# A per-row skewness kernel: row-to-partition mapping, load widths and the closing of the last two blocks

## The chip, the cores and the metric

The kernel runs on one core of a Trainium2 chip. The metric is the device time of one execution in microseconds (us), lower is better. Thirteen runs of the kernel before are at hand, and one profiled execution of it.

The engines named below: TensorE (PE, with its weight loads shown apart as PEld), VectorE (DVE), ScalarE (ACT), GpSimd (POOL) and SyncE (SP), which here only issues DMA transfers. SBUF is the memory on the chip that all of them reach; PSUM is the one into which PE writes.

## The reference

```python
rows, cols = 1024, 8192                      # x is float32, normally distributed
mean = np.mean(x, axis=-1, keepdims=True)
std = np.std(x, axis=-1, keepdims=True)
z = (x - mean) / (std + 1e-8)
return np.mean(z ** 3, axis=-1)              # 1024 numbers
```

For each row the kernel needs three means: m1 of x, m2 of x squared, m3 of x cubed. With var = m2 - m1², the answer is (m3 - 3·m1·(var + m1²/3)) · var^(-1.5); the two inner terms are 3·m1·m2 - 2·m1³ written differently. x is 33.55 MB and is read once.

## The kernel before, in words

The 1024 rows are eight blocks of 128; row 128b+p of x goes to partition p of block b. A block is 8192 columns wide and is loaded in *units*, whose widths are listed in `UNITS`: four for block 0 (512, 1024, 2560, 4096), two each for blocks 1 to 3, then three, four, five, and nine for block 7 (1152 four times, 1024, 896, 896, 512, 256). There are 31 units, so 31 loads, all issued in order by SP. One unit is 128 row pieces, one for each partition. Eight unit buffers rotate (`X_BUFS = 8`): the load of a unit is issued when the unit eight places before it has been read by PE, ACT and DVE.

Work on a unit, cut into slices of at most 2304 columns (`SUB_MAX`), goes in this order:

- ACT squares a slice (`sq`, line 135), with a scale that makes the sum along the row a share of m2. The sum goes to one column of `s2u` (or of `s2l` in block 7).
- DVE multiplies `sq` by x (line 139), and the sum, a share of m3, goes to one column of `s3u` (or `s3l`). DVE waits for ACT's slice.
- PE sums x itself: it transposes each 128 columns and accumulates all of them in one PSUM tile `tp` (line 145). At the end of a block ACT copies `tp` to `tsb` (line 115), and a matmul with a column of 1/8192 leaves m1 of the block in column b of `s1ps` (line 116).

The slices of the last two units of block 7 have their `sq` in PSUM and their cube in a scratch tile `cubes`.

Blocks 0 to 6 are closed together after block 6 (`finish_first_blocks`): two reductions on DVE (line 97), three small ACT instructions (lines 101 to 103), six on POOL. Block 7 is closed at the end: ACT sums `s2l` (line 156), then squares m1, and forms `var`, `nm1` and `v3` from it (lines 160 to 165); POOL raises `var` to the power -1.5 (line 163); DVE reduces `s3l` (line 157), combines it with `v3` and `nm1` (line 166) and multiplies by the power (line 169). The 128x8 tile `skew` is then transposed on PE (line 172), copied out of PSUM by DVE (line 174), and stored by one DMA of eight pieces of 512 bytes (line 175).

The engines run their own instructions in order. A scheduler places the instructions that are written near one another, so the order on an engine may differ a little from that of the source.

Of the kernel before, what the change touches and what calls it, by code (L numbers as in the profile page):

```python
# [8 lines left out]
FP = mybir.dt.float32  # L9
AF = mybir.ActivationFunctionType  # L10
ALU = mybir.AluOpType
X_AXIS = mybir.AxisListType.X


UNITS = [
    [512, 1024, 2560, 4096],
    [4096, 4096],
    [4096, 4096],
    [4352, 3840],
    [3328, 2816, 2048],  # L20
    [2048, 2048, 2048, 2048],
    [1792, 1792, 1664, 1536, 1408],
    [1152, 1152, 1152, 1152, 1024, 896, 896, 512, 256],
]
SUB_MAX = 2304
X_BUFS = 8
SQ_BUFS = 4
PSUM_SQ = 2


def _slices(w):
    n = -(-w // SUB_MAX)
    step = -(-w // n // 128) * 128
    return [(s, min(s + step, w)) for s in range(0, w, step)]


@with_exitstack
def kernel(
    ctx: ExitStack,
    tc: tile.TileContext,  # L40
    x: bass.AP,
    out: bass.AP,
):
    nc = tc.nc
    P = nc.NUM_PARTITIONS
    R, C = x.shape
    NB = R // P
    L = NB - 1
    inv_n = 1.0 / float(C)
    s_scale = float(C) ** -0.5  # L50
    third = (1.0 / 3.0) ** 0.5
    assert len(UNITS) == NB and all(sum(u) == C for u in UNITS)

    xv = x.rearrange("(b p) c -> b p c", p=P)
    ob = out.rearrange("(b p) -> b p", p=P)


    n_sub = [sum(len(_slices(w)) for w in u) for u in UNITS]
    MAXC = max(n_sub[:L])
    NL = n_sub[L]  # L60

    xpool = ctx.enter_context(tc.tile_pool(name="xp", bufs=X_BUFS))
    sqpool = ctx.enter_context(tc.tile_pool(name="sqp", bufs=SQ_BUFS))
    onep = ctx.enter_context(tc.tile_pool(name="onep", bufs=1))
    psum = ctx.enter_context(tc.tile_pool(name="ps", bufs=2, space=bass.MemoryType.PSUM))
    psq = ctx.enter_context(tc.tile_pool(name="psq", bufs=2, space=bass.MemoryType.PSUM))
    psum1 = ctx.enter_context(tc.tile_pool(name="ps1", bufs=1, space=bass.MemoryType.PSUM))

    onesn = onep.tile([P, 1], FP, tag="onesn")
    nc.vector.memset(onesn, inv_n)  # L70
    tiny = onep.tile([P, 1], FP, tag="tiny")
    nc.scalar.activation(out=tiny, in_=onesn, func=AF.Square)  # L72
    ident = onep.tile([P, P], FP, tag="ident")
    make_identity(nc, ident)
    s2u = onep.tile([P, L * MAXC], FP, tag="s2u")
    s3u = onep.tile([P, L * MAXC], FP, tag="s3u")
    nc.vector.memset(s2u, 0.0)
    nc.vector.memset(s3u, 0.0)
    s2l = onep.tile([P, NL], FP, tag="s2l")
    s3l = onep.tile([P, NL], FP, tag="s3l")  # L80
    cubes = onep.tile([P, 512], FP, tag="cubes")
    junk = onep.tile([P, NL], FP, tag="junk")
    expo = onep.tile([P, L], FP, tag="expo")
    nc.gpsimd.memset(expo, -1.5)
    skew = onep.tile([P, NB], FP, tag="skew")
    s1ps = psum1.tile([P, NB], FP, tag="s1ps")

    Tsb = [onep.tile([P, P], FP, tag=f"tsb{i}", name=f"tsb{i}") for i in range(2)]

    def small(name, n):  # L90
        return onep.tile([P, n], FP, tag=name, name=name)

    def finish_first_blocks():

        m2, m3 = small("m2a", L), small("m3a", L)
        for dst, src in ((m2, s2u), (m3, s3u)):
            nc.vector.tensor_reduce(  # L97
                out=dst, in_=src.rearrange("p (b c) -> p b c", c=MAXC), axis=X_AXIS, op=ALU.add
            )
        m1sq, m1sq3, nm1 = small("m1sqa", L), small("m1sq3a", L), small("nm1a", L)  # L100
        nc.scalar.activation(out=m1sq, in_=s1ps[:, 0:L], func=AF.Square)
        nc.scalar.activation(out=m1sq3, in_=s1ps[:, 0:L], func=AF.Square, scale=third)
        nc.scalar.activation(out=nm1, in_=s1ps[:, 0:L], func=AF.Copy, scale=-3.0)
        g = nc.gpsimd
        var, rr = small("vara", L), small("rra", L)
        g.tensor_tensor(out=var, in0=m2, in1=m1sq, op=ALU.subtract)  # L106
        g.tensor_tensor(out=m1sq3, in0=m1sq3, in1=var, op=ALU.add)  # L107
        g.tensor_tensor(out=m1sq3, in0=m1sq3, in1=nm1, op=ALU.mult)  # L108
        g.tensor_tensor(out=m3, in0=m3, in1=m1sq3, op=ALU.add)  # L109
        g.tensor_tensor(out=rr, in0=var, in1=expo, op=ALU.pow)  # L110
        g.tensor_tensor(out=skew[:, 0:L], in0=m3, in1=rr, op=ALU.mult)  # L111

    def close_block(b, tp):
        tsb = Tsb[b % 2]
        nc.scalar.copy(out=tsb, in_=tp)  # L115
        nc.tensor.matmul(out=s1ps[:, b : b + 1], lhsT=tsb, rhs=onesn, start=True, stop=True)  # L116

    for b, widths in enumerate(UNITS):
        last = b == L
        tp = psum.tile([P, P], FP, tag="tp", name=f"tp_{b}")  # L120
        c0 = 0
        j = 0
        for k, w in enumerate(widths):
            xt = xpool.tile([P, w], FP, tag="x", name=f"x_{b}_{k}")
            nc.sync.dma_start(out=xt, in_=xv[b, :, c0 : c0 + w])
            c0 += w
            for s, e in _slices(w):
                i = b * MAXC + j
                a2 = s2l[:, j : j + 1] if last else s2u[:, i : i + 1]
                a3 = s3l[:, j : j + 1] if last else s3u[:, i : i + 1]  # L130
                j += 1
                in_psum = last and k >= len(widths) - PSUM_SQ
                pool = psq if in_psum else sqpool
                sq = pool.tile([P, e - s], FP, tag="sq", name=f"sq_{b}_{k}_{s}")
                nc.scalar.activation(  # L135
                    out=sq, in_=xt[:, s:e], func=AF.Square, scale=s_scale, accum_out=a2
                )
                cube = cubes[:, 0 : e - s] if in_psum else sq
                nc.vector.scalar_tensor_tensor(  # L139
                    out=cube, in0=sq, scalar=1.0, in1=xt[:, s:e],  # L140
                    op0=ALU.mult, op1=ALU.mult, accum_out=a3,
                )
            n = w // P
            for c in range(n):
                nc.tensor.matmul(  # L145
                    out=tp, lhsT=xt[:, c * P : (c + 1) * P], rhs=ident,
                    start=(k == 0 and c == 0), stop=(c0 == C and c == n - 1),
                    is_transpose=True,
                )
        close_block(b, tp)  # L150
        if b == L - 1:
            finish_first_blocks()


    m2, m3 = small("m2l", 1), small("m3l", 1)
    nc.scalar.activation(out=junk, in_=s2l, func=AF.Copy, accum_out=m2)
    nc.vector.tensor_reduce(out=m3, in_=s3l, axis=X_AXIS, op=ALU.add)  # L157
    m1sq, var, nm1, v3 = small("m1sql", 1), small("varl", 1), small("nm1l", 1), small("v3l", 1)
    p1 = s1ps[:, L:NB]
    nc.scalar.activation(out=m1sq, in_=p1, func=AF.Square)  # L160
    nc.scalar.activation(out=var, in_=m1sq, func=AF.Identity, scale=-1.0, bias=m2)  # L161
    rr = small("rrl", 1)
    nc.gpsimd.tensor_tensor(out=rr, in0=var, in1=expo[:, 0:1], op=ALU.pow)  # L163
    nc.scalar.activation(out=nm1, in_=p1, func=AF.Copy, scale=-3.0)
    nc.scalar.activation(out=v3, in_=m1sq, func=AF.Identity, scale=1.0 / 3.0, bias=var)
    nc.vector.tensor_scalar(  # L166
        out=m3, in0=v3, scalar1=nm1, scalar2=m3, op0=ALU.mult, op1=ALU.add
    )
    nc.vector.tensor_tensor(out=skew[:, L:NB], in0=m3, in1=rr, op=ALU.mult)  # L169

    skT_ps = psum1.tile([NB, P], FP, tag="skT")
    nc.tensor.matmul(out=skT_ps, lhsT=skew, rhs=ident, start=True, stop=True, is_transpose=True)  # L172
    skT = small("skT", P)[0:NB, :]
    nc.vector.tensor_copy(out=skT, in_=skT_ps)  # L174
    nc.sync.dma_start(out=ob, in_=skT)


# [28 lines left out]
```

## Time and profile before

| What | Value |
|---|---|
| median of 13 runs | 93.29 us (92.28 to 93.66) |
| profiled execution | 93.07 us |
| its span, first to last instruction | 91.3 us |
| outside the span | 1.8 us |
| instructions | 1437 |
| granted TensorE clock, mean | 0.993 |
| DMA loads | 31, 33.55 MB |
| output store issued at | 89.21 us of the span |

The profile's page gives the busy time of each engine, a strip of 40 slices of the span with the busy share in tenths, and groups of instructions with their mean duration, the idle time just ahead of them, and what ended that idle time. Other views of the same trace are used below: who waited for whom, and the timeline, which lists instructions with start, duration, engine, line, operation, output and inputs, and in brackets the idle time before them with what ended it.

### The profile page before, as it was taken

What the parts mean: (1) busy time and instruction counts of PE and PEld (TensorE: products, weight loads), DVE (VectorE), ACT (ScalarE), POOL (GpSimd) and SP (SyncE); (2) the same over time, 40 slices, a digit from 0 to 9 for tenths busy, and PEclk for the clock granted to TensorE, in tenths of its full rate; (3) what the DMA queues carried; (4) which work ended last, traced back from release to release, by engine and by line L of the source; (5) the groups of instructions that cost most, each with busy time, mean ns of one, the idle gap of its engine ahead of it and who ended that gap; (6) DMA issues with size and microseconds to landing.
All of it is one profiled execution on the core that took longest, in us unless ns stands there. A gap on an engine that the chain in (4) does not pass through costs nothing. (4 is left out here: it accounts for less than half of the span.)

```text
span 91.3 us, 1437 instructions
## 1 busy us (share of the span) xinstructions
PE 68.3 (75%) x529; PEld 60.8 (67%) x529; DVE 73.8 (81%) x91; ACT 69.3 (76%) x101; POOL 9.4 (10%) x14
## 2 busy tenths in 40 slices
PE   0480898979495949779298998887789798989610
PEld 0360897979493939678297897877678687867500
DVE  0142290898989798987969999999999999999960
ACT  6350827969595959779399999977798899999830
POOL 3000000000000000000000000000000000699820
PEclk9999999999999999999999999999999999999997
DMA  1999999999999999999999999999999999992000
GB/s 41 357 346 448 438 438 402 445 438 438 395 445 438 441 408 450 399 424 432 407 428 415 433 409 413 434 403 412 422 417 414 412 409 414 413 364 99 0 0 2
DMA packets 4486, 33.64 MB, mean 369 GB/s; under 512 B 504, under 2 KB 640, under 8 KB 2560
## 3 DMA queue, kind: packets, MB, share of 16 engines
q1 hardware_dynamic: 4480, 33.56, 88.9%
q8 instruction: 4, 0.07, 0.3%
q14 instruction: 2, 0.02, 0.0%
HBM read 33.55 MB, written 0.00 MB: 368 GB/s over the span
## 5 line engine op out<-in xcount | busy, mean ns | idle before, releaser
L139 DVE SCALAR_TENSOR_TENSOR sq<-sq,x 128x2048 f32<-128x2048 f32 (+11 forms) x39 | 71.5, 1884 | 13.9 <-ACT sq L135 13.9
L145 PE MATMUL tp<-ident,x 128*128 128x128 f32 x512 | 65.5, 285 | 15.0 <-DMA x<-in_x_dram 14.7
L135 ACT ACTIVATE sq<-x 128x2048 f32<-128x2048 f32 (+12 forms) x41 | 62.9, 1534 | 17.1 <-DMA x<-in_x_dram 16.1
L145 PEld LDWEIGHTS tp<-ident,x 128*128 128x128 f32 x512 | 59.0, 147 | 20.3 <-DMA x<-in_x_dram 16.8
L106 POOL TENSOR_TENSOR vara<-m2a,m1sqa 128x7 f32<-128x7 f32 x1 | 1.3, 1293 | 77.0 <-DVE m3a L97 77.0
L135 ACT ACTIVATION_READ_ACCUMULATOR sq<-x 128x1 f32 x41 | 7.6, 186 | 0.0
L116 PEld LDWEIGHTS s1ps<-onesn,tsb 128*128 128x128 f32 x16 | 2.4, 188 | 5.5 <-ACT tsb L115 5.5
L116 PE MATMUL s1ps<-onesn,tsb 128*128 128x1 f32 x16 | 3.1, 261 | 3.6 <-ACT tsb L115 3.6
L139 DVE DVE_READ_ACCUMULATOR sq<-sq,x 128x1 f32 x39 | 3.2, 82 | 0.0
L110 POOL TENSOR_TENSOR rra<-vara,expo 128x7 f32<-128x7 f32 x1 | 2.6, 2622 | 0.0
L115 ACT COPY tsb<-tp 128x128 f32<-128x128 f32 x8 | 2.0, 252 | 0.1
L72 ACT ACT_TABLE_LOAD x1 | 1.3, 1283 | 0.7 <-PEq L190 0.7
L172 PE MATMUL skT_ps<-ident,skew 128*8 128x128 f32 x1 | 0.3, 273 | 2.0 <-DVE skew L169 2.0
L172 PEld LDWEIGHTS skT_ps<-ident,skew 128*8 128x8 f32 x1 | 0.1, 83 | 2.1 <-DVE skew L169 2.1
L107 POOL TENSOR_TENSOR m1sq3a<-m1sq3a,vara 128x7 f32<-128x7 f32 x1 | 1.2, 1202 | 0.1
L139 DVE SCALAR_TENSOR_TENSOR cubes<-sq,x 128x512 f32<-128x512 f32 (+1 forms) x2 | 1.1, 554 | 0.1
L108 POOL TENSOR_TENSOR m1sq3a<-m1sq3a,nm1a 128x7 f32<-128x7 f32 x1 | 1.1, 1150 | 0.0
L109 POOL TENSOR_TENSOR m3a<-m3a,m1sq3a 128x7 f32<-128x7 f32 x1 | 0.9, 935 | 0.1
L111 POOL TENSOR_TENSOR skew<-m3a,rra 128x7 f32<-128x7 f32 x1 | 0.9, 933 | 0.1
L70 DVE MEMSET onesn<- 128x1 f32 x1 | 0.1, 59 | 0.8 <-PEq L190 0.8
L163 POOL TENSOR_TENSOR rrl<-varl,expo 128x1 f32<-128x1 f32 x1 | 0.6, 561 | 0.6 <-ACT varl L161 0.6
L174 DVE COPY skT<-skT_ps 8x128 f32<-8x128 f32 x1 | 0.3, 279 | 0.4 <-PE skT_ps L172 0.4
(25 smaller groups left out, 4.4 us busy)
## 6 DMA issues: line engine op xcount, KB each, us to landing
x<-in_x_dram SPq DMA_DIRECT2D x5, 2048.0 KB, 18.8
x<-in_x_dram SPq DMA_DIRECT2D x5, 1024.0 KB, 25.1
x<-in_x_dram SPq DMA_DIRECT2D x4, 576.0 KB, 9.8
x<-in_x_dram SPq DMA_DIRECT2D x1, 2176.0 KB, 34.1
x<-in_x_dram SPq DMA_DIRECT2D x1, 1920.0 KB, 37.6
x<-in_x_dram SPq DMA_DIRECT2D x2, 896.0 KB, 14.8
x<-in_x_dram SPq DMA_DIRECT2D x1, 1664.0 KB, 34.9
x<-in_x_dram SPq DMA_DIRECT2D x1, 1408.0 KB, 31.3
```

Source lines behind the costliest of these rows:

```text
L72: nc.scalar.activation(out=tiny, in_=onesn, func=AF.Square)
L106: g.tensor_tensor(out=var, in0=m2, in1=m1sq, op=ALU.subtract)
L107: g.tensor_tensor(out=m1sq3, in0=m1sq3, in1=var, op=ALU.add)
L108: g.tensor_tensor(out=m1sq3, in0=m1sq3, in1=nm1, op=ALU.mult)
L109: g.tensor_tensor(out=m3, in0=m3, in1=m1sq3, op=ALU.add)
L110: g.tensor_tensor(out=rr, in0=var, in1=expo, op=ALU.pow)
L111: g.tensor_tensor(out=skew[:, 0:L], in0=m3, in1=rr, op=ALU.mult)
L115: nc.scalar.copy(out=tsb, in_=tp)
L116: nc.tensor.matmul(out=s1ps[:, b : b + 1], lhsT=tsb, rhs=onesn, start=True, stop=True)
L135: nc.scalar.activation(out=sq, in_=xt[:, s:e], func=AF.Square, scale=s_scale, accum_out=a2)
L139: nc.vector.scalar_tensor_tensor(out=cube, in0=sq, scalar=1.0, in1=xt[:, s:e], op0=ALU.mult, op1=ALU.mult, accum_out=a3,)
L145: nc.tensor.matmul(out=tp, lhsT=xt[:, c * P : (c + 1) * P], rhs=ident, start=(k == 0 and c == 0), stop=(c0 == C and c == n - 1), is_transp ...
```

## The change

- **Rows.** Partition p of block b now holds row 8p+b. Neighbouring partitions of one load are 8 rows apart in memory (256 KB in place of 32 KB). The eight results of a partition are neighbours in the output, and `skew` is stored directly by one DMA of 128 pieces of 32 bytes. The transpose, the copy and their tiles are gone.
- **Widths.** `UNITS` has 27 units: 4096 wide in blocks 0 to 3, then shrinking, and 1024 to 1408 in block 7, the last one 1152. The last unit alone has its `sq` in PSUM.
- **Row sums on ACT.** In the first unit of blocks 0, 1 and 2 the last 1024 columns are summed by an ACT copy with a row sum (`S1_ACT`, line 159) and no longer by PE: 24 transposes fewer. The two parts of m1 are added by DVE (line 177).
- **Closing.** Blocks 0 to 5 are closed together after block 5, in the same manner as seven were. Blocks 6 and 7 are closed with a chain of six small ACT instructions each (`close_on_act`); for block 6 it is spread between the squares of block 7. The last of the six writes v3·nm1 (the m1 term of the numerator) into a spare column of `s3u`, so that one reduction over `s3u` gives both numerators. One POOL power and one DVE multiplication then serve both blocks.

```diff
 UNITS = [
-    [512, 1024, 2560, 4096],
-    [4096, 4096],
-    [4096, 4096],
-    [4352, 3840],
-    [3328, 2816, 2048],
-    [2048, 2048, 2048, 2048],
-    [1792, 1792, 1664, 1536, 1408],
-    [1152, 1152, 1152, 1152, 1024, 896, 896, 512, 256],
+    [4096, 4096],
+    [4096, 4096],
+    [4096, 4096],
+    [4096, 4096],
+    [3584, 2304, 2304],
+    [2304, 2304, 2048, 1536],
+    [1664, 1792, 1920, 1664, 1152],
+    [1024, 1024, 1152, 1280, 1408, 1152, 1152],
 ]
+S1_ACT = {(0, 0): 1024, (1, 0): 1024, (2, 0): 1024}
-PSUM_SQ = 2
+EARLY = 6
...
-    xv = x.rearrange("(b p) c -> b p c", p=P)
-    ob = out.rearrange("(b p) -> b p", p=P)
+    xv = x.rearrange("(p b) c -> b p c", b=NB)
+    ov = out.rearrange("(p b) -> p b", b=NB)
...
+    def close_on_act(b):
+        m2, m1sq, nm1, v3 = (small(f"{t}_{b}", 1) for t in ("m2", "m1sq", "nm1", "v3"))
+        p1 = s1ps[:, b : b + 1]
+        var = var2[:, b - F : b - F + 1]
+        act = nc.scalar.activation
+        yield act(out=junk, in_=s2u[:, b * K : b * K + K], func=AF.Copy, accum_out=m2)
+        yield act(out=m1sq, in_=p1, func=AF.Square)
+        yield act(out=var, in_=m1sq, func=AF.Identity, scale=-1.0, bias=m2)
+        yield act(out=nm1, in_=p1, func=AF.Copy, scale=-3.0)
+        yield act(out=v3, in_=m1sq, func=AF.Identity, scale=1.0 / 3.0, bias=var)
+        yield act(
+            out=s3u[:, b * K + K - 1 : b * K + K], in_=v3, func=AF.Identity, scale=nm1
+        )
...
+            w_act = S1_ACT.get((b, k), 0)
+            if w_act:
+                nc.scalar.activation(
+                    out=same[:, 0:w_act], in_=xt[:, w - w_act : w], func=AF.Copy,
+                    scale=inv_n, accum_out=s1a[:, b : b + 1],
+                )
+            n = (w - w_act) // P
...
+            if k > 0:
+                next(pending, None)
+                next(pending, None)
...
+        if b == F - 2:
+            nc.vector.tensor_tensor(
+                out=m1a[:, 0:nw], in0=s1ps[:, 0:nw], in1=s1a, op=ALU.add
+            )
+        if b == F - 1:
+            close_first_blocks()
+        if b >= F:
+            pending = close_on_act(b)
+    for _ in pending:
+        pass
+    rr = small("rr2", NB - F)
+    nc.gpsimd.tensor_tensor(out=rr, in0=var2, in1=expo[:, 0 : NB - F], op=ALU.pow)
+    num = small("num2", NB - F)
+    nc.vector.tensor_reduce(
+        out=num, in_=s3u[:, F * K :].rearrange("p (b c) -> p b c", c=K), axis=X_AXIS, op=ALU.add
     )
...
-    nc.tensor.matmul(out=skT_ps, lhsT=skew, rhs=ident, start=True, stop=True, is_transpose=True)
-    skT = small("skT", P)[0:NB, :]
-    nc.vector.tensor_copy(out=skT, in_=skT_ps)
-    nc.sync.dma_start(out=ob, in_=skT)
+    nc.vector.tensor_tensor(out=skew[:, F:NB], in0=num, in1=rr, op=ALU.mult)
+    nc.sync.dma_start(out=ov, in_=skew)
```

## The prediction

> **What bounds the kernel now.** I read the page's strip of 40 slices first, to see which engine is full and when.
>
> ```profile
> DVE  0142290898989798987969999999999999999960
> ...
> DMA  1999999999999999999999999999999999992000
> GB/s 41 357 346 448 438 438 402 445 438 438 395 445 438 441 408 450 399 424 432 407 428 415 433 409 413 434 403 412 422 417 414 412 409 414 413 364 99 0 0 2
> ```
>
> The DMA engines are full from the second slice to the 36th: the loads never pause. DVE has gaps in the first half and none in the second. The waits, asked for two windows (up to 47 us and after), say the same. The columns are the total, how many, and the longest.
>
> ```profile
> DVE sq L139 <- ACT sq L135: 13.2, 9, 3.5
> ```
> ```profile
> DVE sq L139 <- ACT sq L135: 0.7, 1, 0.7
> ```
>
> DVE's waits for ACT are ACT's waits for data, passed on; the last one ends at 47.05. From the timeline, the rows that carry the sums:
>
> ```profile
> 9.43 4.53 PE L145 MATMUL tp<-ident,x 128*128 128x128 f32 x20 [2.52 <-DMA x<-in_x_dram]
> ...
> 45.09 3.50 PE L145 MATMUL tp<-ident,x 128*128 128x128 f32 x30 [1.77 <-DMA x<-in_x_dram]
> ...
> 47.05 2.16 DVE L139 SCALAR_TENSOR_TENSOR sq<-sq,x 128x1920 f32<-128x1920 f32 x1 [0.71 <-ACT sq L135]
> ...
> 59.78 1.97 PE L145 MATMUL tp<-ident,x 128*128 128x128 f32 x16 [0.30 <-DMA x<-in_x_dram]
> ```
> ```profile
> 83.92 1.40 PEld L145 LDWEIGHTS tp<-ident,x 128*128 128x128 f32 x13 [0.33 <-DMA x<-in_x_dram]
> ...
> 85.92 0.24 ACT L115 COPY tsb<-tp 128x128 f32<-128x128 f32 x1
> ...
> 86.63 0.17 ACT L160 ACTIVATE m1sql<-s1ps 128x1 f32<-128x1 f32 x1 [0.27 <-PE s1ps L116]
> ...
> 87.16 0.29 ACT L165 ACTIVATE v3l<-m1sql,varl 128x1 f32<-128x1 f32 x1
> ...
> 87.72 0.16 DVE L157 TENSOR_REDUCE m3l<-s3l 128x1 f32<-128x9 f32 x1
> ...
> 88.38 0.16 DVE L169 TENSOR_TENSOR skew<-m3l,rrl 128x1 f32<-128x1 f32 x1
> 88.59 0.08 PEld L172 LDWEIGHTS skT_ps<-ident,skew 128*8 128x8 f32 x1 [2.08 <-DVE skew L169]
> ...
> 89.21 0.37 SPq L175 DMA_DIRECT2D out_dram<-skT  x1
> ```
>
> A PE row that waited for DMA starts when a unit has landed. 45,056 columns are there at 59.78, 64,768 at 83.92: 24.14 us / 19,712 = 1.2246 ns a column, 512 bytes each, 418 GB/s. Going back on that line, 32,768 columns are due at 44.73 (seen: 45.09) and 4,096 at 9.62 (seen: 9.43), so one line serves the whole kernel, and all 65,536 have landed at 83.92 + 768 × 1.2246 ns = 84.86. DVE's pace is read from starts that follow one another in the timeline: 57.94 to 60.15 for 2048 columns, 79.46 to 80.74 for 1152, so 0.084 us an instruction and 1.038 ns a column, 15% faster than the data. DVE therefore works off the lag that wide units give it. The path is: data up to 45.09, ACT's first slice, DVE without a gap from 47.05 to 87.69 (40.6 us), then a tail of 1.5 us to the store at 89.21 and 2.1 us more to the end of the span.
>
> **The change part by part.**
>
> *Start.* The small first units go. DVE then starts at about 11.5 in place of 4.16. This costs nothing: what covers it is the later wait for data, which DVE has at every unit up to 47.05. What could gain is the stream: slices 2 and 3 run at 357 and 346 GB/s against 440 later, so (83 + 94) GB/s × 2.28 us = 0.40 MB or 0.9 us is lost there. If the small transfers are the reason, it comes back; if it is a run-in of the queue, nothing does. Bounds 0 and -0.9; I take -0.3, nearer to the run-in, since 1152-wide loads later keep 413 GB/s.
>
> *ACT sums three times 1024 columns* (nearest row: 1024-wide square, 1.06 us and 0.19 for its sum). ACT needs 2 × 1.91 for a 4096 unit, which comes every 5.02; 3.82 + 1.1 still fits. PE has 24 transposes fewer (0.12 us each: 32 take 3.71), but PE waits for data there anyway. Both cost nothing; without the cover the three copies would be 3.2 us. The eight buffers need no new wait: SP already waits for a buffer (22 waits for DVE) while the DMA row stays full, and the last seven units hold 8,192 columns, 10 us of stream.
>
> *DVE to the end.* Both kernels have landed 32,768 columns with the second unit of block 3. Taking 45.09 again, ACT's first slice (2048, 1.91) and 0.15 of handing over let DVE start at 47.15. It then has 36,864 columns in 22 instructions: 38.27 + 1.85, plus 0.24 for the two reductions (line 97 before, now after block 5) and 0.12 for line 177: end 87.63. The rest before was 36,608 columns in 25 instructions. So DVE by itself ends where it ended.
>
> *ACT in blocks 6 and 7.* This is the new load. After block 5 and again after block 6, ACT now waits in its own order for PE's `s1ps` before the next square; in the tail of before the same step took 85.92 to 86.63. Queued behind it are the squares, and behind these DVE. For block 6: 0.71 for copy and wait, 0.07, then 0.42 for var, nm1, v3 (v3 started 0.53 after m1sq), 0.08 for the s3u column: 1.3 us. ACT's free time in block 7 is the data's pace less its own: 1024 wide 1.25 - 1.06, 1152 wide 1.41 - 1.17, 1280 and 1408 wide about 0.30 and 0.35, together 1.5 us up to the last unit. So ACT is late by over 1 us at the second unit of block 7 and just on time at the last one. DVE, which by then has no lag left, loses some 0.3 us in short waits. End of the cubes about 87.9. The other bound agrees: last data 84.86, square 1.17, handing over 0.15, cube 1.35 + 0.08: 87.6.
>
> *Tail.* The last square ends at about 86.07, 0.2 us after the last one of before (the 256-wide piece, 85.89). From the `tsb` copy at 86.1, v3 starts 1.24 later (85.92 to 87.16), the new column 0.33 after that and takes 0.29: ready at 87.96. The one reduction starts at 88.0, bounded by ACT and DVE alike (before 87.72). From there: reduce 0.16, gap 0.1, multiply 0.16, 0.04 to the issue: 88.5. Before it was 89.21, since line 166 (0.38 with its gap) and transpose and copy (88.55 to 89.21) stood in between. POOL's power of two columns (0.56 for one) waits for var at 87.3 and is ready at 88.0, hidden. POOL's six for the first blocks move some 9 us earlier, clear of it. Sum: -0.7.
>
> *Store.* 8 pieces of 512 bytes become 128 of 32. The trace has the nearest row on the load side: the first load, 128 pieces of 2 KB on an idle queue, lands 2.6 us after its issue, of which 0.6 us is its 256 KB at 418 GB/s; the other 2.0 is no more than the 2.1 of the store. By that row the piece count costs nothing. The Trainium skill, "DMA: Bandwidth & Descriptors", section "Specifications", speaks against it: a piece under 512 B is written by reading and modifying. Its HBM access latency is 0.2 us on average ("Latency and other measured facts"); with 8 pieces on each of 16 engines one after another my estimate from the page is 1.6 us. Below zero there is little to find: the store must still be issued and land. I take +0.3, near the row.
>
> *Row pitch.* All loads now step 256 KB from partition to partition; the trace has 32 KB alone, at 418 GB/s, and by that row nothing changes. The skill's rule speaks against: the same page, section "Latency and other measured facts", has copies of 128 × 16 KiB tiles at 207 GB/s with a 512 KiB pitch, 164 at 2 MiB, 103 at 4 MiB, and about 214 unhindered. 3.3% of the 80.2 us of stream (33.55 MB at 418) is 2.6 us, an estimate for twice our pitch, so an upper bound; half an effect would be 1.3. No row shows that another pitch is better, but a little gain isn't excluded. I take 0, since the fall is small at 512 KiB and shrinks with the pitch, and keep 2.6.
>
> Sum on the profiled execution: start -0.3, tail -0.7 (the later end of the cubes is in it), store +0.3, pitch 0: -0.7, so the span goes from 91.3 to 90.6 and the time from 93.07 to about 92.4. That execution lies 0.2 below the median of the 13; against 93.29 it is 92.6.
>
> **The rivals.**
>
> *The pitch slows the stream* (slower side). Place: every load. Price: 0.8 us for each percent. It eats the gain at 0.9%, 414 GB/s in place of 418, and is slower by over 0.5% from about 1.5%. At the page's 3.3%: 92.6 + 2.6 = 95.2. For it: the kernel hangs on the stream from end to end, with PE and ACT waiting at unit after unit. Against: the pitch before is a power of two as well and costs nothing visible.
>
> *ACT's chains eat the gain.* If each dependent small instruction costs its 0.33 and the wait for PE 0.7 twice, block 6's closing is 2.1 us against 1.5 free; the last square starts 0.5 us late, everything after it too, and with a store at +0.5 the time is 93.3. For it: order on ACT puts m1sq ahead of block 7's first square. Against: in before, three such ACT instructions (lines 101 to 103) took 0.17 together.
>
> *The start gives its full 0.9 us* and the store costs nothing: 93.29 - 0.7 - 0.9 = 91.7.
>
> **How the numbers follow.** A measurement of this kernel can tell about 0.5% (0.47 us) from no change. Forecast (around 92.6): 0.38, of which 0.05 within 0.5%. Pitch: 0.28, of which 0.03 within. ACT and store: 0.18, of which 0.08 within, 0.08 slower, 0.02 faster. Start in full: 0.16, all faster. Faster 0.33 + 0.02 + 0.16 = 0.51; within 0.16; slower 0.25 + 0.08 = 0.33. The likeliest case alone is 92.0 to 93.1. The range goes from 91.5 (beyond the full start by a little) to 95.2 (the page's pitch figure).
>
> **What would show it.** Right: GB/s near 430 from the second slice; 32,768 columns landed at about 44.8, the last unit at 84.5; DVE full from about 47; short DVE waits in block 7; the reduction on line 190 waiting for ACT's column at about 87.7, 0.5 us from there to the store's issue, and 2.1 to 2.4 more to the end. Wrong: landings drifting behind 1.2246 ns a column (pitch); ACT's squares of block 7 starting over 0.3 us after their data at the last unit (chains); over 2.6 us from the store's issue to the end (store).

## The result, and the profile after

The changed kernel takes 91.46 us (median of 11 runs, 91.37 to 91.65), the kernel before 93.22 (48 runs, 92.06 to 93.91). The medians differ by 1.76 us. The ratio, for which runs over 1.5% above the fastest of the same kernel are left out, is 0.9856, with a 95% interval of 0.9825 to 0.9886: faster by 1.4%, or 1.3 us. The forecast was 0.7 us faster, and the range ended at 91.5, so the direction held and the size did not. The scatter changed as well: 1.85 us before, 0.28 after.

The strip of the changed kernel has the same shape as before. The loads never pause and DVE is full from the middle on.

```profile
DVE  1000498989999199898989999999999999999970
...
DMA  3899999999999999999999999999999999994000
GB/s 95 342 415 437 430 437 430 430 437 415 430 452 394 452 430 415 437 430 414 428 409 413 418 435 418 417 409 421 423 414 412 407 410 417 415 407 165 0 0 2
```

The waits, again up to 47 us and from 47 us on (total, how many, longest):

```profile
DVE sq L152 <- ACT sq L147: 13.4, 8, 9.2
```
```profile
DVE sq L152 <- ACT sq L147: 0.4, 1, 0.4
DVE num L189 <- ACT s3u L128: 0.2, 1, 0.2
```

The 0.4 of the second view is the wait that ends at 46.02 (0.38, in the rows below); its instruction runs on past 47 us, so both views list it. DVE's waits for ACT are thus 13.4 us in all, against 13.9 before (13.2 and 0.7), although DVE's first cube now starts at 10.27 in place of 4.16. The early gap cost nothing. The new wait is the one of the reduction (line 189, in the prediction 190) for ACT's column, and it is 0.2 us. The rows of the timeline that answer to those of before:

```profile
8.28 8.47 PE L165 MATMUL tp<-ident,x 128*128 128x128 f32 x56 [8.28 <-DMA x<-in_x_dram]
...
10.27 2.29 DVE L152 SCALAR_TENSOR_TENSOR sq<-sq,x 128x2048 f32<-128x2048 f32 x1 [9.23 <-ACT sq L147]
```
```profile
43.94 3.71 PE L165 MATMUL tp<-ident,x 128*128 128x128 f32 x32 [1.18 <-DMA x<-in_x_dram]
...
46.02 2.29 DVE L152 SCALAR_TENSOR_TENSOR sq<-sq,x 128x2048 f32<-128x2048 f32 x1 [0.38 <-ACT sq L147]
```
```profile
83.81 1.20 PE L165 MATMUL tp<-ident,x 128*128 128x128 f32 x9 [0.19 <-DMA x<-in_x_dram]
...
85.05 0.27 ACT L174 COPY tsb<-tp 128x128 f32<-128x128 f32 x1
...
86.32 0.29 ACT L127 ACTIVATE v<-m1sq,var 128x1 f32<-128x1 f32 x1
...
86.65 0.30 ACT L128 ACTIVATE s3u<-v,nm 128x1 f32<-128x1 f32 x1
...
86.98 0.17 DVE L189 TENSOR_REDUCE num<-s3u 128x2 f32<-128x16 f32 x1 [0.19 <-ACT s3u L128]
87.25 0.16 DVE L192 TENSOR_TENSOR skew<-num,rr 128x2 f32<-128x2 f32 x1
87.44 0.35 SPq L193 DMA_DIRECT2D out_dram<-skew  x1
```

Read side by side, the two executions differ in these places:

| us | before | after | difference | forecast |
|---|---|---|---|---|
| 4,096 columns landed | 9.43 | 8.28 | -1.15 | -0.3 |
| 32,768 columns landed | 45.09 | 43.94 | -1.15 | -0.3 |
| all landed | 84.86 | 83.81 | -1.05 | -0.3 |
| all landed to the store's issue | 4.35 | 3.63 | -0.72 | -0.7 |
| the store's issue to the end of the span | 2.09 | 2.46 | +0.37 | +0.3 |
| span | 91.3 | 89.9 | -1.4 | -0.7 |

In the first three rows the forecast is off, and the 1.15 us of the first is not simply carried along. In between, at 24,576 columns, the two executions are level. The row of before, then the row of the changed kernel:

```profile
34.19 3.71 PE L145 MATMUL tp<-ident,x 128*128 128x128 f32 x32 [1.18 <-DMA x<-in_x_dram]
```
```profile
34.16 3.71 PE L165 MATMUL tp<-ident,x 128*128 128x128 f32 x32 [2.05 <-DMA x<-in_x_dram]
```

The lead at 32,768 columns, where DVE waits for data for the last time, comes up again after that. The experiments show from what. The two profiled executions (93.07 and 91.72) differ by 1.35; the medians differ by 0.4 more, because the first lies 0.15 below its median and the second 0.26 above.

### The profile page after: what moved, and what is told of

It is laid out like the page before. It is cut to its first block, busy times and chain, and to the rows that moved or that the text cites. A ratio compares the mean times of both kernels' runs of the same rounds, so it can differ in the third digit from the quotient of the medians.

```text
span 89.9 us, 1368 instructions
## 1 busy us (share of the span) xinstructions
PE 64.4 (72%) x504; PEld 58.6 (65%) x504; DVE 72.8 (81%) x80; ACT 72.1 (80%) x106; POOL 11.3 (13%) x14
## 4 chain that ended last, share of the span: by engine, by line
DMA 68%; ACT 18%; issue 5%; DVE 4%; PE 1%; DVEq 0%; ACTq 0%; SPq 0%
DMA x<-in_x_dram 68%; ACT sq L147 14%; DVE sq L152 3%; ACT sqps L147 1%; ACT same L159 1%; PE s1ps L175 1%; ACT tsb L174 0%; ACT s3u L128 0%; ACT v L127 0%; ACT var L125 0%; DVE num L189 0%; ACT m1sq L124 0%; DVE skew L192 0%; ACT nm L126 0%; DVEq L152 0%
## 5 line engine op out<-in xcount | busy, mean ns | idle before, releaser
L152 DVE SCALAR_TENSOR_TENSOR sq<-sq,x 128x2048 f32<-128x2048 f32 (+9 forms) x35 | 70.7, 2071 | 13.5 <-ACT sq L147 13.4
L165 PE MATMUL tp<-ident,x 128*128 128x128 f32 x488 | 61.9, 286 | 17.9 <-DMA x<-in_x_dram 17.9
L165 PEld LDWEIGHTS tp<-ident,x 128*128 128x128 f32 x488 | 56.9, 148 | 21.8 <-DMA x<-in_x_dram 13.4
L147 ACT ACTIVATE sq<-x 128x2048 f32<-128x2048 f32 (+9 forms) x35 | 60.6, 1733 | 11.5 <-DMA x<-in_x_dram 10.4
L110 POOL TENSOR_TENSOR vara<-m2a,m1sqa 128x6 f32<-128x6 f32 x1 | 1.8, 1822 | 67.3 <-DVE m3a L99 67.3
L114 POOL TENSOR_TENSOR rra<-vara,expo 128x6 f32<-128x6 f32 x1 | 3.3, 3265 | 0.0
L159 ACT ACTIVATE same<-x 128x1024 f32<-128x1024 f32 x3 | 3.1, 1042 | 0.0
L111 POOL TENSOR_TENSOR m1sq3a<-m1sq3a,vara 128x6 f32<-128x6 f32 x1 | 1.9, 1867 | 0.1
L152 DVE SCALAR_TENSOR_TENSOR cube<-sqps,x 128x1152 f32<-128x1152 f32 x1 | 1.4, 1350 | 0.0
L113 POOL TENSOR_TENSOR m3a<-m3a,m1sq3a 128x6 f32<-128x6 f32 x1 | 1.2, 1200 | 0.1
## 6 DMA issues: line engine op xcount, KB each, us to landing
x<-in_x_dram SPq DMA_DIRECT2D x1, 960.0 KB, 13.2
```

Source lines behind the costliest of these rows:

```text
L147: nc.scalar.activation(out=sq, in_=xt[:, s:e], func=AF.Square, scale=s_scale, accum_out=s2u[:, j : j + 1],)
L152: nc.vector.scalar_tensor_tensor(out=cube, in0=sq, scalar=1.0, in1=xt[:, s:e], op0=ALU.mult, op1=ALU.mult, accum_out=s3u[:, j : j + 1],)
L159: nc.scalar.activation(out=same[:, 0:w_act], in_=xt[:, w - w_act : w], func=AF.Copy, scale=inv_n, accum_out=s1a[:, b : b + 1],)
L165: nc.tensor.matmul(out=tp, lhsT=xt[:, c * P : (c + 1) * P], rhs=ident, start=(k == 0 and c == 0), stop=(c0 == C and c == n - 1), is_transp ...
```

## The experiments

The first group asks what brought the data 1.15 us earlier. Two parts of the change touch the loads: the wide first units (theory W) and the 256 KB step between partitions (theory P). Each is done alone on the kernel before, and undone alone in the changed kernel.

**b_start**

```diff
-    [512, 1024, 2560, 4096],
+    [4096, 4096],
```

> The kernel before, with block 0 loaded as two units of 4096 in place of 512, 1024, 2560, 4096. Theory W (the wide first units are what brings the data 1.15 us earlier): 4,096 columns landed at about 8.3 in place of 9.43, 32,768 at about 43.9, time 92.1. Theory P (the 256 KB step between partitions brings it): landings as in before, time 93.2.

Measured: 92.16 us (7 runs, 92.08 to 92.25); the kernel before in the same group 92.98. Ratio 0.9923, interval 0.9886 to 0.996. It has 32,768 columns at 43.73, and the first landing at 8.21:

```profile
8.21 2.15 PE L145 MATMUL tp<-ident,x 128*128 128x128 f32 x9 [8.21 <-DMA x<-in_x_dram]
```

**b_pitch**

```diff
-    xv = x.rearrange("(b p) c -> b p c", p=P)
+    xv = x.rearrange("(p b) c -> b p c", b=NB)
```

> The kernel before, with row 8p+b on partition p for the loads alone; the store is as in before, so the 1024 results come out in another order. Theory P: 4,096 columns landed at about 8.3, time 92.1. Theory W: landings as in before (9.43 and 45.09), time 93.2. If the pitch costs anything, the slope of the landings is above 1.2246 ns a column.

Measured: 92.64 (10 runs, 92.15 to 94.6), ratio 0.9962, interval 0.9926 to 0.9999, which just excludes no change; the wide scatter of before stays. The landings are 9.06 and, for 24,576 columns, 34.12: close to the 9.43 and 34.19 of before, with no steeper slope. But 32,768 columns are there at 43.91, as early as in the changed kernel, and not at the 45.09 that theory W expected:

```profile
43.91 3.49 PE L145 MATMUL tp<-ident,x 128*128 128x128 f32 x30 [0.66 <-DMA x<-in_x_dram]
```

**a_start**

```diff
-    [4096, 4096],
+    [512, 1024, 2560, 4096],
...
-S1_ACT = {(0, 0): 1024, (1, 0): 1024, (2, 0): 1024}
+S1_ACT = {(0, 2): 1024, (1, 0): 1024, (2, 0): 1024}
```

> The changed kernel, with block 0 loaded as 512, 1024, 2560, 4096 (the 1024 columns that ACT sums are then the last of the 2560 unit). Theory W: 4,096 columns landed at about 9.4, everything after it 1.1 us later, time 92.6, and runs that scatter by over 1 us as those of before do. Theory P: 91.5 and the narrow scatter of the changed kernel.

Measured: 92.25 (10 runs, 91.69 to 93.12). The first landing is back near 9, and the scatter is back. But at 32,768 columns only 0.19 us of the lateness is left (44.13 against 43.94), where theory W expected 1.1:

```profile
8.98 1.21 PE L165 MATMUL tp<-ident,x 128*128 128x128 f32 x9 [2.12 <-DMA x<-in_x_dram]
```
```profile
44.13 3.71 PE L165 MATMUL tp<-ident,x 128*128 128x128 f32 x32 [1.18 <-DMA x<-in_x_dram]
```

**a_pitch**

```diff
-    xv = x.rearrange("(p b) c -> b p c", b=NB)
+    xv = x.rearrange("(b p) c -> b p c", p=P)
```

> The changed kernel, with row 128b+p on partition p as in before; the store is unchanged, so the 1024 results come out in another order. Theory P: start as in before, time 92.6. Theory W: 91.5, landings as in the changed kernel.

Measured: 91.74 (4 runs, 91.62 to 91.83), first landing 8.29. The narrow scatter stays without the new rows.

In their times all four point to W. Widths alone give 0.8 us between the medians (0.7 by the ratio), and undone they cost 0.6 to 0.8 (against 91.46 to 91.67 for the changed kernel in three groups); the row step gives or takes at most 0.3. How the widths do it can be seen in part from the trace's marks of each load. There are 16, taken here as one for every DMA engine; they carry no engine's number. The first and the last of the 16, for the load that completes 4,096 columns, how many come over 1 us after the first, and the last mark at two later places:

```
kernel    first   last  between  over 1 us   last mark at  last mark at   profiled
          mark    mark           behind      20,480 col.   32,768 col.    run
before    7.79    9.39   1.60       4          29.25         45.04         93.07
b_pitch   7.59    9.02   1.43       2          29.18         43.87         92.29
a_start   7.74    8.94   1.19       4          29.55         44.09         91.88
b_start   7.70    8.08   0.37       0          29.01         43.69         92.08
a_pitch   7.70    8.15   0.45       0          28.94         43.64         91.75
changed   7.46    8.14   0.69       0          29.22         43.90         91.72
```

The first engine is about as early everywhere. With the short first units, two to four engines fall behind by 1.0 to 1.6 us. A load is complete when its last engine is, and the loads follow each other without a pause, so these engines stay behind: in before the marks of the next three loads are still 1.6 us apart. Yet at 20,480 columns all six kernels have a last mark near 29. By then one engine has been set back by some 1.5 us in each of them (the next group shows by what), and a lag of the start on other engines is hidden behind it. It costs time where both fall on the same engine. In before, the trace has such a hold-up at 42.90, 1.09 us long. Twelve of the 16 marks at 32,768 columns lie at 43.32 or earlier; one engine that was late already comes at 45.04. It was due at about 43.3 (33.54 at 24,576 columns, and the others took 9.8 us for the two loads since). In b_pitch and a_start this did not happen. That this chance also makes the scatter of the runs fits, but is not shown: each kernel has one trace.

**a_again and a_fewpe.** The landings of units of 4096 columns come 4.9 us apart, but in the changed kernel there is a step of 6 us and more between 22.85 and 29.2. The page's DMA table has four 16 KB packets of a queue called "instruction", and one of them lies at 26.6 us. a_again is the changed kernel, as the yardstick of the group. a_fewpe takes most of PE's instructions away, and leaves out most of the row sum m1 with them:

```diff
-            n = (w - w_act) // P
+            n = min(2, (w - w_act) // P)
```

> The changed kernel once more, as the yardstick of this group: 91.5, scatter of some 0.3 us, 32,768 columns landed at about 43.9. If the 256 KB pitch cost anything, it would now lie above the 91.74 of the same kernel with rows 128b+p.

> The changed kernel with PE transposing the first two 128-column pieces of each unit only, so that most of the row sum m1 is left out; loads, ACT and DVE are unchanged. Theory F: the four 16 KB instruction packets in the page's DMA table are PE's, each holds one DMA engine up, and a load is complete with its last engine; without them the steps of over 6 us between landings of 4096 units go, and the landings after 25 us come 1.3 to 1.5 us earlier: time 90.0 to 90.4. Rival: the packets cost nothing, 91.5.

Measured: a_again 91.55 (91.35 to 91.68), a_fewpe 90.85 (90.83 to 90.88). PE has 140 instructions in place of 1008, and the queue named q8 is gone. First a_again, then a_fewpe (packets, MB, share of the 16 engines):

```profile
q1 hardware_dynamic: 4032, 33.56, 89.8%
q8 instruction: 4, 0.07, 0.3%
q14 instruction: 2, 0.02, 0.0%
```
```profile
q1 hardware_dynamic: 4032, 33.56, 90.4%
q14 instruction: 2, 0.02, 0.0%
```

The step goes with it; a_again from 22.98 to 28.98, a_fewpe from 22.77 to 27.67:

```profile
22.98 3.71 PE L165 MATMUL tp<-ident,x 128*128 128x128 f32 x32 [2.06 <-DMA x<-in_x_dram]
...
28.98 0.76 PE L165 MATMUL tp<-ident,x 128*128 128x128 f32 x5 [1.47 <-DMA x<-in_x_dram]
```
```profile
22.77 0.69 PE L165 MATMUL tp<-ident,x 128*128 128x128 f32 x2 [4.21 <-DMA x<-in_x_dram]
...
27.67 0.69 PE L165 MATMUL tp<-ident,x 128*128 128x128 f32 x2 [0.18 <-DMA x<-in_x_dram]
```

So PE's own instructions share the DMA engines with the data. One such packet took 1.09 us in a_again, and in the marks of the next load the last engine is 1.98 us behind the first in place of 0.88 (a_fewpe: 0.66 to 0.69 up to 40,960 columns, 1.15 at the end); 32,768 columns landed 1.3 us earlier without them, and 0.7 us of that reached the end (theory F had expected 1.1 or more: by the last landing, 83.68 against 82.75, part of the lead was gone, and the tail took some more). The instructions that the change drops (1058 to 1008) do not take a packet away: four before, four after. PE also reads less of SBUF in a_fewpe, but that is not what moves the landings: where no packet falls, they come 4.9 us apart in both. Short first units without PE's instructions were not run; they would show what the late start costs by itself.

**b_widths** takes all eight lines of `UNITS`; two are shown.

```diff
-    [512, 1024, 2560, 4096],
+    [4096, 4096],
...
-    [1152, 1152, 1152, 1152, 1024, 896, 896, 512, 256],
+    [1024, 1024, 1152, 1280, 1408, 1152, 1152],
...
-PSUM_SQ = 2
+PSUM_SQ = 1
```

> The kernel before with all the widths of the changed kernel (only the last unit's squares in PSUM), old closing, old store. If the start alone counts: as with block 0 alone changed, 92.2. If the later widths count too, 91.8 or less, with DVE ending its cubes before 86.5. If they hurt the old closing (last unit 1152 in place of 256), 92.4 or more.

Measured: 92.34 (10 runs, 92.25 to 92.44), against 92.16 for b_start in another group. The widths of the later blocks gain nothing for the old closing. Its cubes end at 86.74, b_start's at 86.60.

**bs_direct**

```diff
-    [512, 1024, 2560, 4096],
+    [4096, 4096],
...
-    xv = x.rearrange("(b p) c -> b p c", p=P)
-    ob = out.rearrange("(b p) -> b p", p=P)
+    xv = x.rearrange("(p b) c -> b p c", b=NB)
+    ob = out.rearrange("(p b) -> p b", b=NB)
...
-    nc.tensor.matmul(out=skT_ps, lhsT=skew, rhs=ident, start=True, stop=True, is_transpose=True)
-    nc.vector.tensor_copy(out=skT, in_=skT_ps)
-    nc.sync.dma_start(out=ob, in_=skT)
+    nc.sync.dma_start(out=ob, in_=skew)
```

> The kernel before with block 0 as two units of 4096, rows 8p+b and skew stored directly (no transpose, no copy). From the rows: transpose and copy 0.66 us gone, the store's own time 2.09 to 2.46: net -0.3 against 92.16, so 91.85. If the store of 32-byte pieces cost as much as the transpose did: 92.2.

Measured: 91.61 (91.51 to 91.91), 0.55 below b_start (in another group) and not to be told from the changed kernel. The last multiplication and the store's issue follow each other at once:

```profile
87.36 0.16 DVE L169 TENSOR_TENSOR skew<-m3l,rrl 128x1 f32<-128x1 f32 x1
87.54 0.35 SPq L171 DMA_DIRECT2D out_dram<-skew  x1
```

From the issue to the end of the span it takes 2.36 us (89.9 - 87.54), b_start 2.19 (90.3 - 88.11). The 128 pieces of 32 bytes cost 0.2 us, and the transpose and copy that they replace 0.66. With start and direct store the whole gain is there; the new closing, the sums on ACT and the later widths together add nothing that can be told.

**Which short units do it.** Six splits of block 0 in the changed kernel (the 1024 columns that ACT sums are moved to another unit of the block where needed):

```diff
-    [4096, 4096],
+    [2048, 2048, 4096],          # a_2048, a_2048b
+    [512, 3584, 4096],           # a_512
+    [1536, 2560, 4096],          # a_1536
+    [512, 1536, 2048, 4096],     # a_three
+    [512, 1024, 1024, 1536, 4096],   # a_four
+    [1024, 512, 2560, 4096],     # a_order
```

> The changed kernel with block 0 as 2048, 2048, 4096. If only short first pieces of 2 and 4 KB set one DMA engine back at the start: as the changed kernel, 91.5 with a scatter of 0.3. If any split of the first 4096 does it: 4,096 columns landed later than 8.6, runs scattered by over 1 us, median 92 or more.

> The changed kernel with block 0 as 2048, 2048, 4096 once more: 91.3 if the split gains, 91.6 if it was chance.

> The changed kernel with block 0 as 512, 3584, 4096: one short first unit in place of two. If the short pieces themselves set an engine back: 92 or more and scattered. If it takes the run of three growing units (512, 1024, 2560): 91.5 with a scatter of 0.3.

> The changed kernel with block 0 as 1536, 2560, 4096. If a 2560 unit behind a shorter one sets an engine back: 4,096 columns landed at 8.8 or later, 92 or more, scattered by over 1 us. If it takes several short units in a row: 91.5, scatter 0.3.

> The changed kernel with block 0 as 512, 1536, 2048, 4096. If several short units in a row set an engine back: 92 or more, scattered by over 1 us. If the 2560 unit does: 91.5, scatter 0.3.

> The changed kernel with block 0 as 512, 1024, 1024, 1536, 4096. If 1024 right behind 512 sets an engine back: 92 or more, scattered by over 1 us. If it needs the 2560 unit too: 91.6, scatter 0.3.

> The changed kernel with block 0 as 1024, 512, 2560, 4096. If two very short units ahead of the 2560 one set an engine back: 92 or more, scattered by over 1 us, 4,096 columns landed at about 9. If the order 512, 1024 matters: 91.6, scatter 0.3.

| kernel | median, us | runs | scatter | between first and last engine at 4,096 columns |
|---|---|---|---|---|
| a_2048 | 91.32 | 4 | 0.18 | 0.47 |
| a_2048b | 91.48 | 6 | 0.31 | 0.26 |
| a_512 | 91.75 | 4 | 0.24 | 0.79 |
| a_1536 | 91.61 | 4 | 0.08 | 0.26 |
| a_three | 91.56 | 4 | 0.08 | 0.44 |
| a_four | 92.56 | 10 | 1.00 | 1.48 |
| a_order | 91.65 | 10 | 1.66 | 0.70 |

One short unit does no harm that can be told, whether 512 or 1536 wide. 512 followed by 1024 (and, in a_four, another 1024) does: a_four is 1 us slower without any 2560 unit, its trace has four engines over 1 us behind at 4,096 columns, and at 20,480 its last mark is at 30.29, 1.1 us after the changed kernel's. In a_order the profiled run, 91.78, is one of seven below 91.8, and three are at 92.39 to 93.03. So in these runs it takes two units of 1024 columns or less one behind the other. With four runs each, a_512, a_1536 and a_three could have missed a late start that comes now and then. What in the DMA engines does it stays open.

**A version from these findings.** best1 is bs_direct with the m1 term of block 7 as a column, and with later widths chosen by adding up landings, ACT and DVE (below on fewer lines than in the kernel); best2 has block 0 as 2048, 2048, 4096 besides.

```diff
+    [4096, 4096], [4096, 4096], [4224, 3968], [4224, 3968],
+    [3200, 2304, 2688], [2560, 2944, 2688],
+    [2432, 1792, 1408, 1408, 1152],
+    [1408, 1536, 1408, 1152, 1024, 896, 768],
...
-    nc.vector.tensor_scalar(out=m3, in0=v3, scalar1=nm1, scalar2=m3, op0=ALU.mult, op1=ALU.add)
+    nc.scalar.activation(out=s3l[:, NL : NL + 1], in_=v3, func=AF.Identity, scale=nm1)
+    nc.vector.tensor_reduce(out=m3, in_=s3l, axis=X_AXIS, op=ALU.add)
```

> Start, rows and direct store of the changed kernel, the m1 term of block 7 as a column of the third sums, but blocks 0 to 6 closed together as before, and later widths chosen anew by adding up landings, ACT and DVE unit by unit (4224, 3968 in blocks 2 and 3, down to 768 for the last unit). The sums give the last multiplication 0.3 us earlier than in the changed kernel: 91.2. If ACT's wait for PE after block 6 is dearer than the 0.7 assumed: 91.5 to 91.8.

> The changed kernel as the yardstick of this group: 91.5, scatter of 0.3 us.

> The version of the last group with the new later widths, with block 0 as 2048, 2048, 4096. If the split's 0.2 us came from the data: 91.2. If it was chance: 91.4.

Measured: best1 91.41 (6 runs, 91.28 to 91.64), the changed kernel beside it (a_third) 91.67 (6 runs, 91.59 to 91.76); in another group best2 91.35 (91.16 to 91.88). best1 is 0.26 us or 0.3% ahead, under the 0.5% that was set as the bound, and its runs overlap those of a_third. It is hardly better, and best2 is not to be told from it.

## Why the prediction was right or wrong, point by point

- **What bounds the kernel: right.** Data, then DVE without a gap, then the tail. A shift of the data by 1.15 us at 32,768 columns went through to the cubes for the most part: they ended at 87.69 before and 86.80 after.
- **Start: the step that failed.** The prediction bounded this term at 0 and -0.9 and took -0.3. The wide first units alone gave 0.8 us (b_start, medians; 0.7 by the ratio), and the profile has the data 1.15 us earlier where DVE waits for it last. Three things were wrong in it. First, more of the lost bytes came back than -0.3 allows for: up to 9 us the trace's packets add up to 2.53 MB in before, 2.73 in b_start and 2.77 in the changed kernel, and 0.24 MB are 0.6 us at 418 GB/s. The argument for the smaller figure, that 1152-wide loads later keep 413 GB/s, says nothing of the first loads. Second, I had counted bytes over all 16 engines. Such a sum can't show that four of them were 1.3 to 1.6 us behind the first. Third, the prediction let one straight line of landings serve the whole kernel. The line hides a step: 24,576 columns are due on it at 34.70 and came 0.5 us earlier, 32,768 are due at 44.73 and came 0.4 later. The step comes with the packet of PE's instructions at 42.90, which fell on an engine that was late already. The prediction had these packets nowhere.
- **A clue that was left unread.** The 13 runs of before were spread over 1.4 us. The prediction did not ask what varied from run to run.
- **Widths at no cost, first cube at 10.27: right.** DVE waits 13.4 us for ACT's squares in all, 13.9 before.
- **ACT in blocks 6 and 7: right.** 0.3 us of short DVE waits was forecast. The waits view lists none there; the timeline has two gaps of some 0.2 us in all ahead of DVE's cubes at 78.57 and 79.91. ACT's column is 0.2 us late for the reduction.
- **Tail: right.** 4.35 to 3.63 us from the last landing to the store. But bs_direct needs about the same (3.66 us from its last mark, 83.88, to 87.54) with the old closing: the direct store alone is worth as much as all the closing.
- **Store: right.** +0.3 was forecast, the two profiles give +0.37, bs_direct against b_start +0.2. The Trainium skill's rule on pieces under 512 B ("DMA: Bandwidth & Descriptors", "Specifications") points the right way, but the estimate of 1.6 us made from it was far too high.
- **Pitch: right at 0.** With the rows of before, the changed kernel takes 91.74; with its own, 91.46 to 91.67. The slowing that the same page ("Latency and other measured facts") has for a pitch of 512 KiB and more does not show at 256 KiB here: 32,768 columns take 39.87 us after (43.94 to 83.81) and 39.77 before (45.09 to 84.86).

## What to carry to other kernels

A load that all 16 DMA engines share is complete with its slowest engine, so read landings (the start of an engine that waited for data), not GB/s; an engine set back in a queue that never pauses stays behind. Two setbacks cost what the larger one costs while they fall on different engines, and add up where they fall on the same one (45.04 in before), so look at several landings before a difference at one of them is carried forward. Two very short loads at the head of the queue can cost more than the early start that they buy, above all where the engines later wait for the data anyway. A scatter of over 1% between runs of one kernel is a finding to follow before any sum is made.

## What was not expected of the hardware

- PE's instructions are loaded by the DMA engines of the data: four packets of 16 KB in the page's table. Without them the kernel is 0.7 us faster (91.55 to 90.85), and the step of 6.0 us between two landings falls to 4.9. A packet takes about 1.1 us, and what it costs depends on the engine that it falls on: at 42.90 in before the last mark came 1.1 us after all the others.
- Two short loads one behind the other (512 and 1024 columns, pieces of 2 and 4 KB) set two to four of the 16 DMA engines back by 1.0 to 1.6 us in the traces of before, b_pitch and a_start; one short load, or 512 followed by 1536, did not in the runs made.
